# A hybrid encoder layer in float32 on one core: sums, weights and remainders issued at other places

## The chip, the cores and the metric

The kernel runs on one core of a Trainium2 chip. A core has a matrix engine (TensorE, "PE" in the profile), a vector engine (DVE), a scalar engine (ACT), a general engine (GpSimd, "POOL") and an engine that issues DMAs (SyncE, "SP"). Each runs its own queue of instructions in order and waits on semaphores for the others. The metric is the device time of one execution in microseconds (us); the number given for a kernel is the median of its runs.

## The reference

One layer on x of shape 1 x 512 x 1024, all float32:

```python
h = rms_norm(x, attn_norm_g)
xr, gate, q, k, v = jnp.split(h @ w_in, ...)
xr = centred_depthwise_conv(xr, conv_w, conv_b)
h_f = rg_lru(xr, ..., False)
h_b = rg_lru(xr, ..., True)
y_rnn = (h_f + h_b) * jax.nn.gelu(gate)
y_attn = dilated_attention(q, k, v, rel_bias)
mix = jnp.concatenate([rms_norm(y_rnn, norm_rnn_g), rms_norm(y_attn, norm_attn_g)], axis=-1)
x = x + mix @ w_out
h = rms_norm(x, mlp_norm_g)
x = x + jnp.square(jax.nn.relu(h @ w_up)) @ w_down
return rms_norm(x, final_norm_g)
```

d_model is 1024, the hidden width of the MLP 4096; the rnn and the attention group have 512 channels each.

## The kernel before

**Products in three matmuls.** Each float32 operand is split into a rounded part (`hi`, dtype fp32r) and its remainder (`lo`), and a product is hi·hi + hi·lo + lo·hi: three matmuls (`mm3`, lines 329 to 331). For a block of weights, `conv_hi` (line 274) makes `whi` from the raw block on ACT, and `conv_lo` (line 282) makes `wlo` on DVE, as raw minus `whi`. Both are issued three blocks ahead of the block that uses them (`feed`, `dfeed`).

**Seven products for eight.** W_out, W_up and W_down are worked as 2 x 2 quadrants in the manner of Strassen and Winograd: seven products named 11, 21, 22 and s1 to s4, of which s1 to s4 take sums of quadrants. The sums of weights are made by DMA: a quadrant is loaded, and others are accumulated onto it by DMAs that POOL issues (`accum_op=add`). These run on DMA queue q0; the plain loads that SP issues run on q1.

**Order of work.** PE, ACT, DVE and POOL are scheduled by hand: their order is the order of the program text. SP's order is left to the framework's planner. The stages are: x and its columns of W_in (`pxr`), v, the gates, q and k with attention, W_out's rnn half (`wo_thunks`) and attention half (`wo_m`), then for each half of the hidden width W_up (`up_step`, `up_tile`) and W_down (`dmm`).

**x's sums (lines 431 to 441).** x comes in eight row tiles k. DVE adds the squares as tiles arrive (`addsq`, line 374). Before the products of k = 7, PE sums them over the partitions (`col_sums`, line 428), DVE and POOL make the reciprocal root (`rstd_cols`, lines 413 and 416), and PE spreads it to a row later (`rows_of`, line 408), which ACT copies (line 422).

**W_out's attention half (lines 1206 to 1273).** The blocks run in the order `OSEQ` = 11, 21, s2, s3, s4, s1, 22, twelve matmuls each: two row tiles tt, two halves k, three matmuls. For s2, s3 and s4 (`BY_DMA`) the remainder is not made on DVE: ACT writes the negated raw block into a tile, rounded (line 255), and a DMA from POOL adds the raw block to it (line 256), which leaves raw minus its rounded value. This is `conv_neg`; for s2 it is called by `neg_first`, for s3 and s4 inside `conv_hi` of the block before.

**W_down, second half.** 28 blocks j of twelve matmuls: 11 and s1 in turns (j = 0 to 7), s2 and 22 (8 to 15), s3 and 21 (16 to 23), s4 (24 to 27), four blocks q of each. s1's raw tile (`ts`) becomes s2's by one accumulation and s4's by another, each issued in `conv_lo` once the tile has been read (line 311). s3's are loaded by `load_s3` (line 1518) and completed by `sum_s3` (line 1522). The seven products go to PSUM banks that s2, s3 and s4 share with 11; where a product ends, DVE adds the bank to x1n (`add`, line 1657). At j = 8 the last norm's weights `fgt` are loaded as two tiles of 128 rows by 512 (line 1732). `fgt` and most activations are tiles of the ring `g` with 48 slots.

Of the kernel before, what the change touches and what calls it, by code (L numbers as in the profile page):

```python
# [13 lines left out]
FR = mybir.dt.float32r  # L14
# [3 lines left out]
P = 128  # L18
# [91 lines left out]
def hybrid_kernel(ctx: ExitStack, tc, xw, xn, w_in, w_v, w_out, w_up, w_dn, gates, vecs, rel, onehot, fg, out):  # L110
# [121 lines left out]
    def wblock(h, b, q):  # L232
        return w_dn[h, int(b[1]) - 1, (int(b[0]) - 1) * NQ + q]
# [20 lines left out]
    def conv_neg(i, lo):  # L254
        act(lo, raws[i], AF.Copy, scale=-1.0)
        nc.gpsimd.dma_start(lo, raws[i], accum_op=OP.add)
        negs[i] = lo

    def neg_first():
        conv_neg(BY_DMA[0], work.tile([P, 1024], FR, name="tw", tag="tw", bufs=4))  # L260

    def conv_hi(i):
        if i < len(chunks):
            i = swap.get(i, i)
            hi = stream.tile([P, 1024], FR, name="whi", tag="whi", bufs=4)
            if i + 1 in BY_DMA[1:]:
                conv_neg(i + 1, stream.tile([P, 1024], FR, name="wlo", tag="wlo", bufs=4))
            splits[i] = (hi,)
            if i in BY_DMA:
                splits[i] += (negs.pop(i),)  # L270
            if i in ON_DVE:
                nc.vector.tensor_copy(hi, raws[i])
            else:
                act(hi, raws[i], AF.Copy)  # L274

    def conv_lo(i):
        if i < len(chunks):
            i = swap.get(i, i)
            r = raws.pop(i)
            if i not in BY_DMA:  # L280
                lo = stream.tile([P, 1024], FR, name="wlo", tag="wlo", bufs=4)
                nc.vector.tensor_tensor(lo, r, f(splits[i][0]), op=OP.subtract)  # L282
                splits[i] += (lo,)
            c = chunks[i]
            if isinstance(c, tuple) and c[0] in ("o", "r"):
                if c[1][0] != "s":
                    emit_dma()
                elif c == ("r", "s2"):
                    nc.gpsimd.dma_start(r, oblock("21", 0), accum_op=OP.add)
                    raws[C_WO + RSEQ.index("s4")] = r  # L290
            elif isinstance(c, tuple) and len(c) == 4:
                h, kind, f0 = c[:3]
                if kind == "t1" and cq[h, f0, "t2"] not in raws:
                    nc.gpsimd.dma_start(r, ublock(h, "22", f0), accum_op=OP.add)
                    raws[cq[h, f0, "t2"]] = r
                elif kind == "22":
                    t = raws[cq[h, f0, "t3"]]
                    nc.vector.tensor_tensor(t, t, r, op=OP.add)
                elif kind in ("t2", "21"):
                    held[kind] = r  # L300
                    if len(held) == 2:
                        t = held.pop("t2")
                        nc.vector.tensor_tensor(t, t, held.pop("21"), op=OP.add)
                        raws[cq[h, f0, "t4"]] = t
                        emit_dma()
                if kind in ("11", "22"):
                    emit_dma()
            elif isinstance(c, tuple) and c[1][0] == "s":
                nxt = {"s1": ("s2", "22"), "s2": ("s4", "21")}.get(c[1])
                if nxt:  # L310
                    nc.gpsimd.dma_start(r, wblock(c[0], nxt[1], c[2]), accum_op=OP.add)
                    raws[cd_[c[0]] + {"s2": 2 * NQ + 2 * c[2], "s4": 6 * NQ + c[2]}[nxt[0]]] = r
            else:
                emit_dma()

# [12 lines left out]
    def mm3(o, a, b, first, last, on=False):  # L328
        nc.tensor.matmul(o, lhsT=a[0], rhs=b[0], start=bool(first), stop=False, skip_group_check=on)  # L329
        nc.tensor.matmul(o, lhsT=a[0], rhs=b[1], start=False, stop=False, skip_group_check=on)  # L330
        nc.tensor.matmul(o, lhsT=a[1], rhs=b[0], start=False, stop=bool(last), skip_group_check=on)  # L331
# [60 lines left out]
    def hk(k):  # L392
        return (h_hi[:, k, :], h_lo[:, k, :])

    def wk(c, k):
        if c < 3:
            return tuple(t[:, c * P:(c + 1) * P] for t in w3[k])
        hi, lo = splits[c]
        return (hi[:, k * P:(k + 1) * P], lo[:, k * P:(k + 1) * P])
# [11 lines left out]
    def rstd_cols(ssc, n):  # L411
        v = small("rv", 4)
        nc.vector.tensor_scalar(v, ssc, 1.0 / n, EPS, op0=OP.mult, op1=OP.add)
        r = consts.tile([P, 4], FT, name="rcol_%d" % st["rc"])
        st["rc"] += 1
        nc.gpsimd.tensor_tensor(r, v, mhalf, op=OP.pow)
        return r
# [7 lines left out]
    def col_sums(ss, tag):  # L425
        pc = ps_("pcs", tag)
        for tt in range(4):
            nc.tensor.matmul(pc[:, tt:tt + 1], lhsT=ss[:, tt * P:(tt + 1) * P], rhs=ones[:, 0:1], start=True, stop=True)
        return pc[:, 0:4]

    pxr = {t: ps_("pxr", "pj") for t in range(3)}
    for k in range(KD):
        if k == KD - 1:
            rcol = rstd_cols(col_sums(sqx[0], "et"), D)
        if k < 4:
            for i, (a, b) in enumerate(((0, 0), (0, 1), (1, 0))):
                for t in range(3):
                    nc.tensor.matmul(pxr[t], lhsT=wk(t, k)[a], rhs=hk(k)[b], start=k == 0 and i == 0, stop=False)
            continue
        for t in range(3):  # L440
            mm3(pxr[t], wk(t, k), hk(k), False, k == KD - 1)


    relt = consts.tile([NB3, P], FT, name="relt")
# [470 lines left out]
    def o_part(w, tt, k):  # L915
        if w in ("21", "s4"):
            c = slice((w == "s4") * TH + tt * P, (w == "s4") * TH + (tt + 1) * P)
            return [t[:, c] for t in osp[k]]
        return [t[:, k * TH + tt * P:k * TH + (tt + 1) * P] for t in osp[w]]
# [283 lines left out]

    hb, hm, po = {}, {}, {}

    def wo_m(w, tt, k):
        b, tag = {"21": ("c", "pj"), "s1": ("b", "gs"), "22": ("b", "gs")}.get(w, ("a", "et"))
        new = w in ("11", "21", "s1")
        if new and tt == 0 and k == 0:
            po[b] = [ps_("pwo", tag) for _ in range(2)]  # L1210
        hi, lo = splits[C_WA + OSEQ.index(w)]
        sl = slice(k * S, (k + 1) * S)
        mm3(po[b][tt], o_part(w, tt, k), (hi[:, sl], lo[:, sl]), k == 0 and new, k == 1, True)


    def wo_x(w, tt):
# [25 lines left out]
    o_hi2(1)  # L1242
    o_sum("s1", 1)
    o_sum("s2", 1)
    o_his("s2")
    o_sum("22", 1)
    o_lo2(1)
# [20 lines left out]
    for w in OSEQ:  # L1268
        for i in range(4):
            tt, k = i // 2, i % 2  # L1270
            wo_m(w, tt, k)
            if k == 1:
                wo_x(w, tt)
            if i in BES[w]:
                BES[w][i]()
        if w in ("s3", "s4", "s1"):
            load_t(0, {"s3": "t1", "s4": "t2", "s1": "t3"}[w], 4)
# [238 lines left out]
    def load_s3(half, q):  # L1516
        t = work.tile([P, 1024], FT, name="tw", tag="tw", bufs=4)
        nc.sync.dma_start(t, wblock(half, "12", q))
        raws[cd_[half] + 4 * NQ + 2 * q] = t

    def sum_s3(half, q):
        nc.gpsimd.dma_start(raws[cd_[half] + 4 * NQ + 2 * q], wblock(half, "22", q), accum_op=OP.add)

# [2 lines left out]
    for half in range(2):  # L1526
# [170 lines left out]
        for j in range(7 * NQ):  # L1697
            _, w, q = seq[j]
            if q == 0:
                if w in dtag:  # L1700
                    dst[w] = [ps_("pd", dtag[w]) for _ in range(2)]
                else:
                    dst[w] = dst["s1" if w == "22" else "11"]
            if w == "s4" and half == 1:
                break
            for tt in range(2):
                for k2 in range(2):
                    dmm(j, dst[w], tt, k2)
                    dfeed(j, 2 * tt + k2)
                if q == NQ - 1:  # L1710
                    evac(w, tt, dst[w][tt])
            if w == "s1":
                del opsplit[w, q]
                load_s3(half, q)
            if j in S3_AT:
                for x in S3_AT[j]:
                    sum_s3(half, x)
            if half == 0 and j == 16:
                load_t(1, "t1", 0)
            if half == 0 and j == 22:  # L1720
                load_t(1, "t3", 0)
            if half == 0 and j >= HJ:
                h_load(j - HJ)
            if half == 0 and j >= HJ + 2:
                h_hi(*HSEQ[j - HJ - 2])
                h_lo(*HSEQ[j - HJ - 2])
            if half == 1 and j in (4 * NQ, 4 * NQ + 1):
                fin_other(j - 4 * NQ)
            if half == 1 and j == 2 * NQ:
                fgt = [g_("fgt") for _ in range(2)]  # L1730
                for n in range(2):
                    nc.sync.dma_start(fgt[n], bass.AP(tensor=fg.tensor, offset=fg.offset + n * S, ap=[[0, P], [1, S]]))
# [89 lines left out]
```

## Time and profile before

| | |
|---|---|
| median of 3 runs | 529.97 us (529.26 to 530.29) |
| profiled execution | 530.81 us |
| its span, first to last instruction | 529.0 us |
| mean granted TensorE clock | 0.996 |
| PE busy | 519.8 us (98%) |
| DVE, ACT, POOL busy | 431.3, 361.3, 67.5 us |
| q1 (loads), q0 (accumulations) | 74.66 MB, 31.76 MB |

A row of a timeline gives the start in us, the duration in us, engine, line, operation, what is written <- what is read, shape and count; in square brackets the idle time of the engine before it and what ended it. A row of waits gives who waited <- for whom: us in total, times, longest. Matmuls are pipelined, so their durations overlap: how far one starts after another is what counts.

### The profile page before, as it was taken

Reading aid. Unit: us, or ns where it says so; the run is one execution under the profiler, and the core shown is the slowest. Engines: PE = TensorE matmul, PEld = TensorE weight load, DVE = VectorE, ACT = ScalarE, POOL = GpSimd, SP = SyncE. Lnnn points to the kernel's source line nnn. Section 1 sums busy time; section 2 is a strip of 40 time slices with the busy share of each in tenths; the row PEclk is TensorE's granted clock in tenths of the full one; section 3 lists DMA queues with packets and bytes.
Section 4 is the critical chain, followed back from the end, with each engine's and each line's share of the span. In section 5 each row is a group of like instructions: output and inputs, shape, how many; then the busy total and the mean of one; then the engine's idle time right before and its main releaser. Section 6 shows DMA issues by size and latency. Waiting matters only on the chain.

```text
span 529.0 us, 9183 instructions
## 1 busy us (share of the span) xinstructions
PE 519.8 (98%) x3495; PEld 446.4 (84%) x3495; DVE 431.3 (82%) x710; ACT 361.3 (68%) x569; POOL 67.5 (13%) x96
## 2 busy tenths in 40 slices
PE   9999999999999999999999999999999999999995
PEld 8766888787877878899999888889999999887884
DVE  5898588887789897898779987789666978885995
ACT  7567977776878957585578655565476687655654
POOL 3340000001002121001300132001101300322000
PEclk9999999999999999999999999999999999999998
DMA  8788155586478999948495899976977596799504
GB/s 305 259 247 210 40 157 164 169 156 183 82 241 206 276 237 248 356 150 199 119 234 129 244 265 273 287 281 160 315 225 180 130 233 193 179 270 260 166 1 159
DMA packets 35884, 108.30 MB, mean 205 GB/s; under 512 B 4125, under 2 KB 7226, under 8 KB 35840
## 3 DMA queue, kind: packets, MB, share of 16 engines
q1 hardware_dynamic: 26144, 74.66, 41.1%
q0 software_dynamic: 8784, 31.76, 31.9%
q10 hardware_dynamic: 912, 1.30, 1.3%
q8 instruction: 27, 0.44, 0.3%
q14 instruction: 17, 0.14, 0.1%
HBM read 98.24 MB, written 4.21 MB: 194 GB/s over the span
## 4 chain that ended last, share of the span: by engine, by line
PE 81%; issue 7%; DMA 6%; DVE 3%; ACT 1%; POOL 1%; SPq 0%; DVEq 0%; POOLq 0%; ACTq 0%
PE pu L329 10%; PE pu L330 10%; PE pu L331 10%; PE pd L329 8%; PE pd L330 8%; PE pd L331 8%; DMA wraw<-in_w_dn_dram 3%; PE pqk L329 3%; PE pqk L330 3%; PE pqk L331 3%; DMA wlo<-ws 2%; PE pv L329 2%; PE pg L519 1%; PE pv L330 1%; PE pv L331 1%
## 5 line engine op out<-in xcount | busy, mean ns | idle before, releaser
L282 DVE TENSOR_TENSOR wlo<-wraw,whi 128x1024 fp32r<-128x1024 f32 x72 | 87.9, 1221 | 30.0 <-ACT whi L274 29.9
L274 ACT ACTIVATE whi<-wraw 128x1024 fp32r<-128x1024 f32 x69 | 72.9, 1058 | 46.2 <-PE pd L331 18.2
L329 PE MATMUL pd<-whi,ah 128*128 128x512 f32 (+1 forms) x195 | 75.3, 386 | 0.9 <-ACT ah L1434 0.9
L330 PE MATMUL pd<-wlo,ah 128*128 128x512 f32 (+1 forms) x195 | 75.3, 386 | 0.0
L331 PE MATMUL pd<-whi,al 128*128 128x512 f32 (+1 forms) x195 | 75.2, 386 | 0.0
L274 ACT ACTIVATE whi<-tw 128x1024 fp32r<-128x1024 f32 x40 | 42.2, 1058 | 31.2 <-PE pu L330 8.9
L330 PE MATMUL pu<-hl,whi 128*128 128x256 f32 x224 | 63.4, 283 | 0.0
L331 PE MATMUL pu<-hh,wlo 128*128 128x256 f32 x224 | 63.4, 283 | 0.0
L329 PE MATMUL pu<-hh,whi 128*128 128x256 f32 x224 | 63.4, 283 | 0.0
L282 DVE TENSOR_TENSOR wlo<-tw,whi 128x1024 fp32r<-128x1024 f32 x40 | 48.9, 1223 | 15.6 <-ACT whi L274 15.6
L329 PE MATMUL pu<-h2h,whi 128*128 128x256 f32 (+1 forms) x200 | 60.1, 301 | 0.0
L331 PE MATMUL pu<-h2h,wlo 128*128 128x256 f32 (+1 forms) x200 | 60.0, 300 | 0.0
L330 PE MATMUL pu<-h2l,whi 128*128 128x256 f32 (+1 forms) x200 | 60.0, 300 | 0.0
L329 PEld LDWEIGHTS pd<-whi,ah 128*128 128x128 f32 x195 | 36.6, 188 | 8.6 <-ACT ah L1434 1.3
L329 PEld LDWEIGHTS pu<-hh,whi 128*128 128x128 f32 x224 | 43.0, 192 | 0.0
L330 PEld LDWEIGHTS pu<-hl,whi 128*128 128x128 f32 x224 | 43.0, 192 | 0.0
L331 PEld LDWEIGHTS pu<-hh,wlo 128*128 128x128 f32 x224 | 43.0, 192 | 0.0
L331 PEld LDWEIGHTS pd<-whi,al 128*128 128x128 f32 x195 | 36.6, 188 | 7.4
L330 PEld LDWEIGHTS pd<-wlo,ah 128*128 128x128 f32 x195 | 36.6, 188 | 7.2
L274 ACT ACTIVATE whi<-ts 128x1024 fp32r<-128x1024 f32 x24 | 25.5, 1061 | 22.4 <-PE pd L331 19.3
L331 PEld LDWEIGHTS pu<-h2h,wlo 128*128 128x128 f32 x200 | 38.3, 191 | 1.3
L329 PEld LDWEIGHTS pu<-h2h,whi 128*128 128x128 f32 x200 | 38.3, 191 | 1.3
(286 smaller groups left out, 1226.8 us busy)
## 6 DMA issues: line engine op xcount, KB each, us to landing
wraw<-in_w_up_dram SPq DMA_DIRECT2D x25, 512.0 KB
ts<-in_w_dn_dram POOLq DMA_DIRECT2D x24, 512.0 KB, 10.7
wraw<-in_w_dn_dram SPq DMA_DIRECT2D x24, 512.0 KB
tw<-in_w_up_dram SPq DMA_DIRECT2D x15, 512.0 KB
tw<-in_w_up_dram POOLq DMA_DIRECT2D x15, 512.0 KB, 8.9
wraw<-in_w_in_dram SPq DMA_DIRECT2D x13, 512.0 KB
ts<-in_w_dn_dram SPq DMA_DIRECT2D x8, 512.0 KB
tw<-in_w_dn_dram SPq DMA_DIRECT2D x8, 512.0 KB
```

The source lines that it names most:

```text
L274: act(hi, raws[i], AF.Copy)
L282: nc.vector.tensor_tensor(lo, r, f(splits[i][0]), op=OP.subtract)
L329: nc.tensor.matmul(o, lhsT=a[0], rhs=b[0], start=bool(first), stop=False, skip_group_check=on)
L330: nc.tensor.matmul(o, lhsT=a[0], rhs=b[1], start=False, stop=False, skip_group_check=on)
L331: nc.tensor.matmul(o, lhsT=a[1], rhs=b[0], start=False, stop=bool(last), skip_group_check=on)
L519: nc.tensor.matmul(pg[2 * d + j][halves[b ^ d]], lhsT=gwr[t][halves[b], c], rhs=xc[t][halves[b]], start=True, stop=True)
```

## The change

Four places are edited. The sums of x's squares are issued after the products of column tile 0 at k = 7, not before all three. In W_out's attention half, s3's remainder is begun right after the sums for s2 have been issued, and for s2, s3 and s4 the matmuls with the weights' remainder come after those with the rounded weights. In the second half of W_down, the accumulations that make s4's weights leave `conv_lo` and stand at j = 15 to 18 of the program. The load of `fgt` stands at j = 0 instead of j = 8.

```diff
+    def neg_next(i):
+        conv_neg(i, stream.tile([P, 1024], FR, name="wlo", tag="wlo", bufs=4))
+
     def conv_hi(i):
...
-            if i + 1 in BY_DMA[1:]:
-                conv_neg(i + 1, stream.tile([P, 1024], FR, name="wlo", tag="wlo", bufs=4))
+            if i + 1 == BY_DMA[2]:
+                neg_next(i + 1)
...
                 if nxt:
-                    nc.gpsimd.dma_start(r, wblock(c[0], nxt[1], c[2]), accum_op=OP.add)
                     raws[cd_[c[0]] + {"s2": 2 * NQ + 2 * c[2], "s4": 6 * NQ + c[2]}[nxt[0]]] = r
+                    if (c[0], c[1]) != (1, "s2"):
+                        nc.gpsimd.dma_start(r, wblock(c[0], nxt[1], c[2]), accum_op=OP.add)
...
     for k in range(KD):
-        if k == KD - 1:
-            rcol = rstd_cols(col_sums(sqx[0], "et"), D)
...
             mm3(pxr[t], wk(t, k), hk(k), False, k == KD - 1)
+            if k == KD - 1 and t == 0:
+                rcol = rstd_cols(col_sums(sqx[0], "et"), D)
...
-    def wo_m(w, tt, k):
+    def wo_m(w, tt, k, late=False):
...
-        mm3(po[b][tt], o_part(w, tt, k), (hi[:, sl], lo[:, sl]), k == 0 and new, k == 1, True)
+        if not late:
+            mm3(po[b][tt], o_part(w, tt, k), (hi[:, sl], lo[:, sl]), k == 0 and new, k == 1, True)
+            return
+        oh, ol = o_part(w, tt, k)
+        for x in (oh, ol):
+            nc.tensor.matmul(po[b][tt], lhsT=x, rhs=hi[:, sl], start=False, stop=False, skip_group_check=True)
+        if k == 1:
+            for k2 in range(2):
+                nc.tensor.matmul(po[b][tt], lhsT=o_part(w, tt, k2)[0], rhs=lo[:, k2 * S:(k2 + 1) * S],
+                                 start=False, stop=k2 == 1, skip_group_check=True)
...
     o_sum("s1", 1)
     o_sum("s2", 1)
+    neg_next(BY_DMA[1])
     o_his("s2")
...
-            wo_m(w, tt, k)
+            wo_m(w, tt, k, w in ("s2", "s3", "s4"))
...
+    def sum_s4d(q):
+        nc.gpsimd.dma_start(raws[cd_[1] + 6 * NQ + q], wblock(1, "21", q), accum_op=OP.add)
...
-            if half == 1 and j == 2 * NQ:
+            if half == 1 and 15 <= j < 15 + NQ:
+                sum_s4d(j - 15)
+            if half == 1 and j == 0:
                 fgt = [g_("fgt") for _ in range(2)]
```

## The prediction

> **What bounds the kernel now.** I read the busy times of the page first, then TensorE's waits, then the timelines of all engines around each wait.
>
> ```profile
> PE 519.8 (98%) x3495; PEld 446.4 (84%) x3495; DVE 431.3 (82%) x710; ACT 361.3 (68%) x569; POOL 67.5 (13%) x96
> PE pwarm L155 <- DVE epsb L146: 1.0, 1, 1.0
> PE pd L329 <- ACT ah L1434: 0.9, 1, 0.9
> PE pwo L330 <- DMA wlo<-ws: 0.6, 1, 0.6
> PE pcs L428 <- DVE sqx L374: 0.3, 1, 0.3
> ```
>
> TensorE (PE) is busy for 519.8 of 529.0 us. Inside the program it waits three times, once at each of three places, and all four parts of the change are aimed at those places: the sums of x's squares (pcs), W_out's block s3 (pwo), and the first s3 block of the second down projection (pd). The change takes no matmul away, so what can be won is these three stalls and nothing else. How long each is in truth has to be read from start to start, because the ends of matmuls are modelled: matmuls of this size start every 0.227 us (190.55 less 190.33, say, in the rows below).
>
> **Part 1, x's sums one column tile later.** The first fence has PE, the second DVE, POOL and ACT at the same place.
>
> ```profile
> 19.45 0.39 PE L331 MATMUL pxr<-h_hi,w3l 128*128 128x512 f32 x1
> 20.18 1.05 PE L428 MATMUL pcs<-ones,sqx 128*128 128x1 f32 x8 [0.34 <-DVE sqx L374]
> ...
> 23.92 0.60 PE L408 MATMUL prow<-ident,rcol 128*128 128x128 f32 x4
> ```
>
> ```profile
> 18.65 1.48 DVE L374 TENSOR_TENSOR sqx<-sqx 128x512 f32<-128x512 f32 x2
> 21.27 0.16 DVE L413 TENSOR_SCALAR rv<-pcs 128x4 f32<-128x4 f32 x1 [1.15 <-PE pcs L428]
> 21.51 1.97 POOL L416 TENSOR_TENSOR rcol<-rv,mhalf 128x4 f32<-128x4 f32 x1 [10.10 <-DVE rv L413]
> 24.70 0.58 ACT L422 ACTIVATE rrow<-prow 128x512 f32<-128x512 f32 x1
> ```
>
> Before, PE could have started the sums at 19.45 + 0.227 = 19.68, but DVE finishes the last add at 18.65 + 1.48 = 20.13, so they start at 20.18: 0.50 us lost, with a handover of 0.05. After, three matmuls of tile 0 run in between (their operands are made by DVE ahead of that last add), and the sums start at 19.45 + 4 x 0.227 = 20.36, when the add is done. The 0.50 is gone, but the sums are 0.18 later, and a chain hangs on them: rv on DVE, the power on POOL, then the transposes prow on PE. POOL ended at 21.51 + 1.97 = 23.48 and will end at 23.66; with the handover prow may start at 23.71. PE will be there at 23.92 - 0.50 = 23.42. **So a new wait of about 0.29 us takes the place of the old one**, on PE, with everything of PE behind it. The next in the chain, rrow on ACT at 24.70, follows a conversion that keeps ACT busy until then, so it does not move. Net: 23.92 - 23.71 = 0.21 us. Bounds: 0.50 if POOL's power is shorter than it shows (POOL's spans are rough), and -0.2 if the handover from POOL is 0.4 us longer than that from DVE. I take 0.21, since it uses the rows as they stand.
>
> **Part 2, W_out.** Block s3 needs its remainder wlo, which ACT (negation) and POOL (an accumulating DMA) make. The first fence is PE, the second ACT, the third POOL, with the landing times of that DMA.
>
> ```profile
> 190.33 0.39 PE L331 MATMUL pwo<-whi,ol 128*128 128x512 f32 x1
> 190.55 0.39 PE L329 MATMUL pwo<-whi,oh 128*128 128x512 f32 x1
> 191.53 0.50 PE L330 MATMUL pwo<-wlo,oh 128*128 128x512 f32 x1 [0.58 <-DMA wlo<-ws]
> ...
> 194.42 0.39 PE L330 MATMUL pwo<-wlo,oh 128*128 128x512 f32 x1
> ```
>
> ```profile
> 180.33 0.63 ACT L896 ACTIVATE oh<-at 128x512 fp32r<-128x512 f32 x1
> 181.25 0.63 ACT L890 ACTIVATE oh<-osum 128x512 fp32r<-128x512 f32 x1 [0.29 <-DVE osum L909]
> 181.79 1.05 ACT L255 ACTIVATE wlo<-ws 128x1024 fp32r<-128x1024 f32 x1
> ...
> 184.88 1.05 ACT L255 ACTIVATE wlo<-ws 128x1024 fp32r<-128x1024 f32 x1
> ```
>
> ```profile
> 183.13 0.86 POOL L256 DMA_DIRECT2D wlo<-ws  x1 [9.97 <-ACT wlo L255]
> 186.22 0.86 POOL L256 DMA_DIRECT2D wlo<-ws  x1 [2.22 <-ACT wlo L255]
> DMA to landing us min/median/max: 7.8/8.1/8.4
> ```
>
> The stall is 191.53 - 190.55 - 0.227 = 0.75 us. The two DMAs landed at 183.13 + 8.4 = 191.5 (s3) and 186.22 + 7.8 = 194.0 (s4); the second was in time by 0.4 us only, because PE had been held at s3.
>
> The negation for s3 moves ahead of one ACT instruction and into ACT's idle 0.29 us: it can start when the oh of 180.33 ends, near 180.9, 0.9 us sooner, and the DMA with it. Its output slot is no new wait: of the four wlo tiles two belong to W_out's rnn blocks that PE has left by then. What is behind it on ACT, the oh of s2, starts about 0.6 us later and is wanted by PE three blocks on, so that is hidden.
>
> The other half is the order of matmuls. For s2, s3 and s4 the remainders come last within each pair of row tiles: 2 + 2 matmuls with hi, then 2 with lo, six as before, so no time of its own; and each of the 3495 matmuls has a weight load of its own (3495 PEld), so pairing gives nothing to lose. The first use of lo goes from the 2nd to the 5th matmul of a block, 3 x 0.227 = 0.68 us later. For s3: wanted at 190.55 - 0.21 + 4 x 0.227 = 191.25, landed near 190.6; if the DMA did not come sooner at all it would land at 191.5, a wait of 0.25. For s4, without the stall: its first matmul at 190.55 - 0.21 + 12 x 0.227 = 193.06, lo wanted at 193.97, landed at 194.0 if unmoved; its negation starts up to 0.29 sooner, since ACT's idle time is filled. So **s4 is what is late next**, by 0.0 to 0.1 us at worst, as its block loses the delay it had been living on. I take 0.75 for the part; bounds 0.45 and 0.75.
>
> **Part 3, second half's sums and the last norm's weights.** PE, then ACT, DVE, the chain of waits, SP, and the DMA queues (packets, MB, share) in 470 to 486 us:
>
> ```profile
> 488.39 0.39 PE L331 MATMUL pd<-whi,al 128*128 128x512 f32 x1
> 489.64 0.47 PE L329 MATMUL pd<-whi,ah 128*128 128x512 f32 x1 [0.87 <-ACT ah L1434]
> 486.52 1.06 ACT L274 ACTIVATE whi<-wraw 128x1024 fp32r<-128x1024 f32 x1 [4.29 <-DMA wraw<-in_w_dn_dram]
> 487.61 1.23 DVE L282 TENSOR_TENSOR wlo<-wraw,whi 128x1024 fp32r<-128x1024 f32 x1 [4.04 <-ACT whi L274]
> 488.75 0.74 DVE L1657 SCALAR_TENSOR_TENSOR x1n<-pd,nr,x1n 128x512 f32<-128x512 f32 x1
> 470.07 16.35 DMA wraw<-in_w_dn_dram
> 467.43 0.50 SPq L1732 DMA_DIRECT2D fgt<-in_fg_dram x1
> q0 software_dynamic: 640, 2.31, 72.4%
> q1 hardware_dynamic: 638, 1.92, 33.1%
> ```
>
> PE was free at 488.39 + 0.227 = 488.62 and went on at 489.64: 1.02 us lost. The page names ACT, but by the code the first matmul of s3 reuses the PSUM bank of s2, which DVE adds into x1n (488.75 to 489.49); that add stands in DVE's queue behind the remainder of weight block (21, 0) (487.61), which waits for whi on ACT (486.52), which waits for the load wraw. **So the load, 16.35 us for 512 KB, is the cause, through the head of two queues.** PE doesn't need that block until block 17; the harm is in what stands behind it. A landing 1.02 us sooner ends the whole stall.
>
> Why 16 us: for all of 470 to 486 both queues were full and took turns, 640 packets of sums (q0) against 638 of loads (q1), so loads advance at 638 / 16 = 40 packets per us. One load has 144 packets, from this row of 446 to 453 us, where 1.05 MB is two loads of 512 KB:
>
> ```profile
> q1 hardware_dynamic: 288, 1.05, 36.8%
> q0 software_dynamic: 49, 0.14, 10.0%
> ```
>
> So each load takes 144 / 40 = 3.6 us there, and 16.35 is this load and three to four ahead of it. One of those ahead is fgt (467.43), 128 rows of 2 KB, which counts as many packets as a full load. Moved to block 0, near 446 us, it meets DMA engines with half their time free, and the load lands about 3.6 us sooner, near 482.8: over three times what is needed. The s4 accumulations come on top: two of the four stood in q0 ahead of sums that s3 wants. The Trainium skill, page "DMA: Bandwidth & Descriptors", section "Queues, rings and completion order", says that each engine goes round-robin between queues packet by packet; 640 against 638 agrees. By that rule taking sums out of q0 brings a load nothing while q0 stays full, and the sum would be fgt's 3.6 us alone; by shares of bytes it would be up to 3.6 more. Either way the stall is covered. I take 1.02; bounds 0 (nothing sooner) and 1.02.
>
> What it costs: the moved sums have no wait on blocks 15 to 18; POOL runs its queue in order, so they go out right behind the last sum of s3. They must land before s4's weights are converted:
>
> ```profile
> 481.08 1.79 POOL L311 DMA_DIRECT2D ts<-in_w_dn_dram x2 [0.31 <-DVE al L1439]
> ts<-in_w_dn_dram POOLq DMA_DIRECT2D x3, 512.0 KB, 13.7
> 503.55 1.06 ACT L274 ACTIVATE whi<-ts 128x1024 fp32r<-128x1024 f32 x1 [1.14 <-PE pd L331]
> ```
>
> The last sum of before was issued at about 482 and lands 13.7 us later, near 496. The queue holds the same sums in another order, so all are in by then; the first is wanted at 503.55 - 2 = 501.5. Cover: 5 us. If it were gone, each us beyond would cost PE a us. The two loads fgt cost SP 0.5 us each at a place where the queues are half idle: nothing.
>
> **Sum.** 0.21 + 0.75 + 1.02 = 1.98 us. Between the three places PE has no other wait, and loads there are issued when PE's and DVE's progress frees a buffer, so a gain is carried on to the end. Span 529.00 - 1.98 = 527.02; the profiled execution took 530.81, 1.81 more than its span, so 528.83. It was 0.84 slower than the median of three, 529.97, from which I forecast **527.99 us**.
>
> **Rivals.**
> 1. *The load stays late.* SP is the one engine whose order is left to a planner, so fgt may not go out at block 0; and loads of (21, 0) behind two s3 loads may still meet a full q0. Against it: the 3.6 us. Then only parts 1 and 2 pay: 529.97 - 0.96 = 529.0. Chance 0.14.
> 2. *The full stretch moves.* Sums bunched behind s3's keep q0 full, every load at 476 to 495 goes on at 40 packets per us, and the stall comes back at a later DVE add. For it: 640 against 638 packets, turn about. The Trainium skill's page "DMA: Bandwidth & Descriptors", same section, has this turn-taking as its rule. Against it: before, q0 was as full, and the view of waits has one wait of pd, not two. If a stall of 1 us came back and part 1 paid nothing, 529.97 - 0.75 = 529.2. Chance 0.12.
> 3. *Slower: SP is held at fgt.* fgt takes two tiles of ring g (48). If these were not free at block 0, SP would stand at its head, and behind it all weight loads. Counted in the code, 32 tiles are alive there (8 x1n, 11 a, 9 as, 2 ah, 2 al), which speaks against it; so does fgt's issue of before without any wait. Weights are converted three blocks ahead (3 x 12 x 0.227 = 8.2 us), so it costs nothing up to a hold of some 8 us, then a us for each us. At 12 us: 529.97 - 0.96 + 4 = 533. Chance 0.10.
>
> **How the numbers follow.** Forecast 0.64 (own range 527.2 to 528.8: all stalls gone with part 1 at its upper end, 2.27 us, and 0.5 for the spread of medians, half of the runs' 529.26 to 530.29, down to part 2 at its lower end with part 1 at nothing, 1.47, and the same 0.5), rivals 0.14, 0.12, 0.10. The range must take in rivals 1 and 2 with the spread of the medians: 527.2 to 529.8. A measurement here can tell about 0.2%, 1.06 us: faster means below 528.9. Faster: 0.64 and a fifth of rivals 1 and 2, 0.69. Slower 0.10. Within: 0.21.
>
> **What would show it.** Part 1: pcs waits for nothing, prow for POOL by about 0.3 us. Part 2: the negation of s3 at about 180.9, no wait of pwo, or one under 0.3 us at s4. Part 3: fgt issued near 446, the load of (21, 0) in under 13 us, no wait at the first pd of s3; s4 sums issued together after the last of s3, landed before 498. It is wrong if PE has a new wait over 0.5 us anywhere, above all between 450 and 515 us, or if fgt stands on SP with a long wait.

## The result, and the profile after

| | before | after |
|---|---|---|
| median of 22 runs each, side by side | 530.0 us (528.97 to 531.75) | 529.14 us (528.47 to 530.58) |
| ratio | | 0.9984, 95% interval 0.9977 to 0.9991 |
| profiled execution, its span | 530.81, 529.0 us | 529.17, 527.4 us |

The change is faster by 0.16%: 0.9984 x 530.0 is 0.85 us less, with an interval from 0.48 to 1.22. The forecast was 1.98 less; the time is inside its range, and the gain below the 0.2% that it took as the bound of what can be told. The two profiled executions differ by 1.64 us, twice as much as the medians; that difference is the thread of what follows.

The page of after, busy times and the chain that ended last, and below it the one line that the view of PE's waits has beside the first wait of before (who waited <- for whom: us, times, longest):

```profile
PE 519.1 (98%) x3495; PEld 445.8 (85%) x3495; DVE 431.2 (82%) x710; ACT 361.1 (68%) x569; POOL 68.7 (13%) x96
...
PE 97%; DMA 1%; DVE 1%; POOL 0%; ACT 0%; SPq 0%; issue 0%; DVEq 0%; ACTq 0%
```

```profile
PE pxr L440 <- ACT w3h L368: 0.8, 1, 0.8
```

All three waits (pcs, pwo, pd) are gone. There is a new one of 0.8 us at the very start, for x's second tile (pxr), ahead of everything that was edited. The prediction had named a new wait of over 0.5 us anywhere as a sign that it is wrong; a second profile of the changed kernel ("after again", below) lists no such wait, and nothing suggests that this one is of the change's making.

**Part 1 after**, the timeline of PE and then of POOL:

```profile
7.62 0.98 PE L440 MATMUL pxr<-h_hi,w3h 128*128 128x512 f32 x3 [0.76 <-ACT w3h L368]
...
20.71 0.94 PE L432 MATMUL pcs<-ones,sqx 128*128 128x1 f32 x8
...
23.47 0.40 PE L335 MATMUL pxr<-h_hi,wlo 128*128 128x512 f32 x1
23.96 0.65 PE L412 MATMUL prow<-ident,rcol 128*128 128x128 f32 x4
```

```profile
21.94 1.96 POOL L420 TENSOR_TENSOR rcol<-rv,mhalf 128x4 f32<-128x4 f32 x1 [10.56 <-DVE rv L417]
```

The sums pcs wait for nothing. prow starts when POOL's power has ended (21.94 + 1.96 = 23.90, start 23.96), and PE was there 0.49 - 0.227 = 0.27 us before (23.47 to 23.96). So the old wait was exchanged for a new one, as forecast. But prow starts at 23.96, against 23.92 before: the start had held PE up.

**Part 2 after**, the timelines of ACT, POOL, SP and PE, and the landing times of the two accumulating DMAs:

```profile
180.42 0.63 ACT L900 ACTIVATE oh<-at 128x512 fp32r<-128x512 f32 x1
180.96 1.04 ACT L255 ACTIVATE wlo<-ws 128x1024 fp32r<-128x1024 f32 x1
...
182.29 0.87 POOL L256 DMA_DIRECT2D wlo<-ws  x1 [9.71 <-ACT wlo L255]
...
183.58 0.33 SPq L241 DMA_DIRECT2D wraw<-in_w_up_dram  x1
...
191.56 0.62 PE L1225 MATMUL pwo<-wlo,oh 128*128 128x512 f32 x2
```

```profile
DMA to landing us min/median/max: 5.3/6.0/6.6
```

The negation starts at 180.96 where 180.9 was forecast. Its DMA lands in 5.3 us, not in 8.4: at 187.6, four us before the first matmul that wants it (191.56). The issue moved by 0.84 us, the landing by 3.9. What went through the DMA queues in the 3 us from the issue (packets, MB, share of 16 engines), before in 183.1 to 186.1 us and then after in 182.3 to 185.3:

```profile
q1 hardware_dynamic: 90, 0.35, 56.8%
q0 software_dynamic: 15, 0.01, 2.0%
```

```profile
q0 software_dynamic: 112, 0.39, 69.1%
q1 hardware_dynamic: 33, 0.08, 7.1%
```

Before, SP's load on q1 went first and the accumulation on q0 hardly moved; the two did not take turns. After, the accumulation goes first.

**Part 3 after**, the timelines of SP, POOL and ACT, then the DMA queues in 470 to 486 us (packets, MB, share):

```profile
444.98 0.95 SPq L1751 DMA_DIRECT2D fgt<-in_fg_dram  x2
...
469.54 0.33 SPq L241 DMA_DIRECT2D wraw<-in_w_dn_dram  x1
...
478.79 3.93 POOL L1536 DMA_DIRECT2D ts<-in_w_dn_dram  x4
...
482.84 1.06 ACT L277 ACTIVATE whi<-wraw 128x1024 fp32r<-128x1024 f32 x1 [1.14 <-PE pd L335]
```

```profile
q0 software_dynamic: 542, 1.98, 66.4%
q1 hardware_dynamic: 611, 2.23, 36.6%
```

fgt goes out at block 0 without a wait. The load of block (21, 0), issued at 469.54, is there when ACT wants it: the conversion at 482.84 waits for PE, where before it waited for the load (at 486.52). So the load took 13.3 us at most, where it took 16.35. The four s4 sums go out together, 478.79 to 482.7; by the trace the last of them starts at 480.95 and lands 15.8 us later, at 496.8.

Nearly all that the prediction said of the places was there; whether the load took under 13 us, as it said, the trace doesn't tell. What was wrong is the amount.

### The profile page after: what moved, and what is told of

Read it like the earlier page. It is cut to its first block, busy times and chain, and to the rows that moved or that the text cites. A ratio compares the mean times of both kernels' runs of the same rounds, so it can differ in the third digit from the quotient of the medians.

```text
span 527.4 us, 9182 instructions
## 1 busy us (share of the span) xinstructions
PE 519.1 (98%) x3495; PEld 445.8 (85%) x3495; DVE 431.2 (82%) x710; ACT 361.1 (68%) x569; POOL 68.7 (13%) x96
## 3 DMA queue, kind: packets, MB, share of 16 engines
HBM read 98.24 MB, written 4.21 MB: 194 GB/s over the span
## 4 chain that ended last, share of the span: by engine, by line
PE 97%; DMA 1%; DVE 1%; POOL 0%; ACT 0%; SPq 0%; issue 0%; DVEq 0%; ACTq 0%
PE pu L333 10%; PE pu L334 10%; PE pu L335 10%; PE pd L333 10%; PE pd L335 10%; PE pd L334 10%; PE pqk L333 3%; PE pqk L335 3%; PE pqk L334 3%; PE pt L845 2%; PE pav L932 2%; PE pv L333 2%; PE pg L523 1%; PE pn L791 1%; PE pv L334 1%; PE pv L335 1%
```

## The experiments

Two theories. **Fixed**: each stall is in every execution as the first profile shows it, and something new gives half of it back. **Come and go**: when a DMA lands, and so how long PE stalls, differs from execution to execution; the first profile of before was a slow draw, and the sum of its stalls isn't what the kernel usually loses.

### The kernel before once more, and each part alone

The kernel before, with no edit:

> The kernel before, unchanged. Theory A (the three stalls of the first profile, 0.50 + 0.75 + 1.02 us, are there in every execution, and the gain is lost somewhere in the changed kernel): this profile shows the same three waits within 0.1 us each. Theory B (the profiled execution was a slow draw, 530.81 against a median of 530.0, because the landing of DMAs differs from execution to execution): one or more of the three waits is shorter by 0.3 us or more, and TensorE's start on x differs too. Time: ratio 1.000 in both.

Part 1 alone:

```diff
-        if k == KD - 1:
-            rcol = rstd_cols(col_sums(sqx[0], "et"), D)
...
+            if k == KD - 1 and t == 0:
+                rcol = rstd_cols(col_sums(sqx[0], "et"), D)
```

> x's sums one column tile later, alone. Theory A: -0.2 us, sums without a wait, and a wait of 0.3 us at the row of roots. Theory B, for this part: what TensorE loses at the start (a wait for x's second tile, 0.76 us in the changed kernel's profile, none in the one before) makes it arrive later at the sums, so that there was little to win: 0.0 to -0.2 us. The waits at W_out's s3 (up to 0.75) and at the first s3 block of the down projection (up to 1.0) stay.

Part 2 alone (both halves):

```diff
-            if i + 1 in BY_DMA[1:]:
+            if i + 1 == BY_DMA[2]:
...
+    neg_next(BY_DMA[1])
...
-            wo_m(w, tt, k)
+            wo_m(w, tt, k, w in ("s2", "s3", "s4"))
```

> W_out alone: s3's negation sooner and remainders last for s2, s3, s4. Theory A: -0.75 us. Theory B: what the wait at s3 is in a usual execution, between 0 and 0.75. In both: no wait of the W_out products in the profile, the waits at x's sums and at the down projection stay.

Part 3 alone (both halves):

```diff
+                    if (c[0], c[1]) != (1, "s2"):
+                        nc.gpsimd.dma_start(r, wblock(c[0], nxt[1], c[2]), accum_op=OP.add)
...
+            if half == 1 and 15 <= j < 15 + NQ:
+                sum_s4d(j - 15)
-            if half == 1 and j == 2 * NQ:
+            if half == 1 and j == 0:
```

> Second half's sums for s4 and the last norm's weights at other blocks, alone. Theory A: -1.0 us. Theory B: what the wait at the first s3 block is in a usual execution, between 0 and 1.0. In both: no wait there in the profile, the load of weight block (21, 0) is in under 13 us, the waits at x's sums and W_out's s3 stay.

| | median (range), us | ratio to before, 95% interval |
|---|---|---|
| before, in the same comparison (35 runs) | 529.51 (528.62 to 531.14) | |
| before again | 529.95 (528.55 to 532.44) | 1.0008, 0.9994 to 1.0022 |
| part 1 | 529.28 (528.89 to 532.55) | 1.0001, 0.9987 to 1.0015 |
| part 2 | 529.13 (528.55 to 530.76) | 0.9996, 0.9984 to 1.0007 |
| part 3 | 528.92 (528.27 to 529.32) | 0.9987, 0.9977 to 0.9996 |

Part 3 alone brings most of what the whole change brings. Its 11 runs spread over 1.05 us, the 35 of before over 2.52. The views of waits tell more; first that of before again, then that of part 2:

```profile
PE pwo L330 <- DMA wlo<-ws: 0.5, 1, 0.5
PE pd L329 <- ACT ah L1434: 0.3, 1, 0.3
```

```profile
PE pd L332 <- ACT ah L1447: 0.9, 1, 0.9
```

The same code as before shows no wait at pcs now, and one of 0.3 us at pd in place of 0.9. Part 1's view lists none at pwo or pd, which it doesn't touch, and part 3's none at pcs or pwo, though both theories had these stay; in part 2's, pd is as bad as in the first profile. That speaks for stalls that come and go.

### The two halves of part 3

fgt alone, the other half being left as before:

```diff
-            if half == 1 and j == 2 * NQ:
+            if half == 1 and j == 0:
```

> Of the change only the two loads fgt at block 0; the s4 sums stay where they were. Theory 'turns' (the two DMA queues take turns packet by packet, so a load is late by the packets of its own queue ahead of it): fgt was 144 packets in front of the load of block (21, 0), so with it gone that load lands about 3.6 us sooner, in about 12 to 13 us instead of 16, and no pd of s3 waits; time as with the whole of part 3, 0.5 to 0.7 us under before. Rival 'sums' (the sums crowd the loads out, so it is the two s4 sums in the other queue that count): the load still takes over 15 us and pd waits 0.3 to 1.1 us in the profile, time within 0.2 us of before.

The s4 sums alone (in the expectation, "block 6" is the place of before, j = 8):

```diff
+                    if (c[0], c[1]) != (1, "s2"):
+                        nc.gpsimd.dma_start(r, wblock(c[0], nxt[1], c[2]), accum_op=OP.add)
...
+            if half == 1 and 15 <= j < 15 + NQ:
+                sum_s4d(j - 15)
```

> Of the change only the four s4 sums together behind the last sum of s3; fgt stays at block 6. Theory 'turns': the sums' queue is as full as before at 470 to 486 us, loads go on at 40 packets per us with fgt among them, the load of block (21, 0) takes 15 us or more, pd waits 0 to 1.1 us as in the executions of before, time within 0.2 us of before. Rival 'sums': the load takes under 13 us, pd waits for nothing, time 0.5 to 0.7 us under before.

Each half ends the stall by itself: neither profile has a wait at pd, and in both the conversion of block (21, 0) waits for PE and not for the load. The timelines of ACT, fgt alone first, then the s4 sums alone:

```profile
482.29 1.06 ACT L274 ACTIVATE whi<-wraw 128x1024 fp32r<-128x1024 f32 x1 [1.14 <-PE pd L331]
```

```profile
482.62 1.06 ACT L274 ACTIVATE whi<-wraw 128x1024 fp32r<-128x1024 f32 x1 [1.14 <-PE pd L332]
```

The queues in 470 to 486 us, in the same order:

```profile
q0 software_dynamic: 596, 2.18, 68.3%
q1 hardware_dynamic: 599, 2.19, 36.7%
```

```profile
q0 software_dynamic: 465, 1.71, 55.6%
q1 hardware_dynamic: 938, 2.87, 47.5%
```

Without fgt the queues still take turns (596 to 599), and the load is early because less stands ahead of it. Without the two s4 sums q0 runs empty for part of the time (2 packets start on it from 478 to 480 us by the trace, beside 292 on q1), and the loads get 938 packets through in place of 638. So 'turns' was right for fgt and wrong for the sums: it took for granted that q0 stays full. 'sums' was wrong in holding fgt for harmless. In time, fgt alone has a median of 528.87 us (528.17 to 529.73) and the s4 sums alone 528.90 (528.34 to 529.74), against 529.25 of before. The ratios are 0.9997 (0.9989 to 1.0006) and 0.9990 (0.9980 to 1.0000): for fgt alone the time by itself tells nothing, and neither median reaches the 0.5 to 0.7 us under before that was expected, so that the verdict on both halves rests on the profiles.

### A third profile of before

No edit:

> The kernel before once more, for a third profile of it and as a measure of what a difference between two like kernels may be. Theory 'intermittent' (the stalls at pcs, pwo and pd depend on when DMAs land, which differs from execution to execution): ratio within 0.15% of 1, and a profile in which the three stalls are again of other sizes than 0.50, 0.75 and 1.02 us, some of them 0. Rival 'fixed': 0.50, 0.75 and 1.02 within 0.1 us.

529.58 us (528.67 to 532.41), ratio 1.0005 (0.9988 to 1.0021). Its view of waits lists none of pcs, pwo or pd. PE's timeline has a small one at W_out, at s4 and not at s3; below it stands ACT's timeline with the conversion of block (21, 0):

```profile
192.74 0.47 PE L329 MATMUL pwo<-whi,oh 128*128 128x512 f32 x1
193.35 0.50 PE L330 MATMUL pwo<-wlo,oh 128*128 128x512 f32 x1
```

```profile
484.79 1.06 ACT L274 ACTIVATE whi<-wraw 128x1024 fp32r<-128x1024 f32 x1 [3.46 <-DMA wraw<-in_w_dn_dram]
```

s3's DMA had landed in 7.1 us, so that s4 was the late one, by 193.35 - 192.74 - 0.227 = 0.38 us: what the prediction had as late next. The load landed near 484.8, 1.7 us sooner than in the first profile, and pd lost 0.2 us in place of 1.02. 'Come and go' (in the expectation, 'intermittent') holds.

### The two halves of part 2

The negation sooner, the order of matmuls left:

```diff
-            if i + 1 in BY_DMA[1:]:
+            if i + 1 == BY_DMA[2]:
...
+    neg_next(BY_DMA[1])
```

> Of the change only the negation for W_out's block s3 sooner; the remainders stay in their places among the matmuls. Theory 'ahead of the load': the accumulating DMA now goes out before the load of the next weight block (182.3 against 183.5 us) and not behind it, so that it lands in about 5.3 us instead of 7.0 to 8.4, near 187.5, three us before it is wanted; s4's lands near 192.5, before it is wanted near 193; first pwo to first pxt takes 15.26 to 15.32 us. Rival 'as predicted': the landing moves by the 0.9 us of the issue alone, to 189 to 190.6, and s4's stays at 192.6 to 194.0 and costs up to 0.5 us. Time 0.2 to 0.5 us under before in the one case, 0 to 0.4 in the other.

The remainders late, the negation left:

```diff
-            wo_m(w, tt, k)
+            wo_m(w, tt, k, w in ("s2", "s3", "s4"))
```

> Of the change only the remainders of s2, s3 and s4 last within their blocks; the negation stays where it was. Both theories: the DMA for s3 goes out at about 183 behind the load and lands in 7.0 to 8.4 us, 189.5 to 191.5, and is wanted near 191.2: a wait of 0 to 0.3 us at s3 and none or 0.1 at s4; first pwo to first pxt 15.26 to 15.6 us. Time 0.1 to 0.4 us under before. If lateness did not matter at all, as where the sums of the page are off by more than this, 15.7 us or more as in before.

The landing times, the negation sooner first, then the remainders late:

```profile
DMA to landing us min/median/max: 5.3/5.9/6.6
```

```profile
DMA to landing us min/median/max: 7.0/7.3/7.6
```

Neither waits at pwo. With the negation sooner, the DMA goes out at 181.82 and SP's load of the next block at 183.11, by their timelines; before, they went out at 183.13 and 183.49, and POOL's issuing instruction ran until 184.0. In all six profiles with the sooner negation s3's DMA lands in 5.3 us; in the eight without, in 7.0 to 8.4. So 'ahead of the load' holds: the issue moved by 0.9 us and the landing by up to 4. That the load is what it passes is read from the order of issues and from the packets shown above; why q0 hardly moves even after 184.0 stays open, and a kernel with the load moved instead was not tried. Of the late remainders the profile shows little: s3's DMA landed at 182.57 + 7.0 = 189.6, in time for the old order too, whose place for it is the second matmul of s3, at 190.23; s4's landed at 185.66 + 7.6 = 193.3, 0.1 us behind the old place at 193.20.

In time the two are 529.32 us (528.48 to 532.61; ratio 0.9998, 0.9984 to 1.0011) and 529.27 (528.70 to 530.14; 0.9995, 0.9986 to 1.0004), against 529.61: nothing that can be told. The profiled execution of the first was one of its longest, 532.61 us, and shows one way in which the kernels without part 3 come to such a tail. The chain that ended last, then PE's timeline, then windows (us, PE busy, PEld, DVE, ACT, POOL, granted clock, DMA share, GB/s):

```profile
469.06 17.56 DMA wraw<-in_w_dn_dram
```

```profile
487.38 0.39 PE L334 MATMUL pd<-whi,al 128*128 128x512 f32 x1
489.85 0.47 PE L332 MATMUL pd<-whi,ah 128*128 128x512 f32 x1 [2.08 <-ACT ah L1438]
...
490.65 0.63 PE L332 MATMUL pd<-whi,ah 128*128 128x512 f32 x1
491.07 0.63 PE L333 MATMUL pd<-wlo,ah 128*128 128x512 f32 x1
```

```profile
488.00:490.60 2.60, 0.75 (x3) 0.67 (x4) 2.60 (x4) 1.77 (x3) 0.00 (x0) 1.00 1.07 279
490.60:494.00 3.40, 3.40 (x9) 2.64 (x8) 3.40 (x5) 0.24 (x1) 0.00 (x0) 0.50 1.05 260
494.00:496.00 2.00, 2.00 (x10) 1.65 (x9) 1.17 (x3) 2.00 (x5) 0.00 (x0) 1.00 0.83 256
```

The load took 17.56 us, PE stood still for 489.85 - 487.38 - 0.227 = 2.24 us, and right after that the granted clock was 0.50 for 3.4 us: matmuls start every 0.42 to 0.43 us. The down projection lost 3.93 us in all. Four of the executions of the kernels without part 3 took 532.4 us or more, and of all whose clock is on record only these have a mean granted clock of 0.995 or less. So a slow stretch is likely in all four; where it fell, only this profile shows.

### The wait at prow, and the changed kernel again

The whole change, and prow one group of matmuls later:

```diff
-    xmm((0,))
+    xmm((0, 1))
     rstd = row_tile(rcol, "et")
...
-    xmm((1, 2, 3, 4))
+    xmm((2, 3, 4))
```

> The whole change, and the transposes of the root row (prow) behind one more group of matmuls. If the wait of 0.27 us at prow is in every execution, as the rows of after have it (the chain DVE, POOL, PE is all compute, no DMA in it): prow waits for nothing and the time is 0.2 to 0.3 us under that of the changed kernel, 528.6 to 528.9. Rival: at the start PE is bound by the landing of x, by 0 to 0.9 us that differ from execution to execution, and the wait at prow is only what the start leaves: no difference within 0.15 us.

The same kernel again, and the changed kernel, side by side:

> The whole change with the transposes of the root row one group of matmuls later, beside the changed kernel on one chip. If the 0.27 us at prow is in every execution: median 0.15 to 0.3 us below the changed kernel's, no wait at prow. If it is only what the start leaves: within 0.15 us of it.

> The changed kernel once more, beside the three below on one chip. Theory 'intermittent': PE's time in W_out (first pwo to first pxt) and in the second down projection (first to last pd) is again 15.29 and 233.00 us within 0.05, since all that could be late there lands with room; what differs is the first stretch alone (first pxr to first pbias, 46.2 to 47.4 us so far). Time 528.6 to 529.2, ratio 0.998 to 0.999. Rival: the stalls of the two later stretches come back in some executions, 0.2 us or more over those sums.

PE's timeline with prow later:

```profile
23.37 0.39 PE L335 MATMUL pxr<-h_hi,wlo 128*128 128x512 f32 x1
23.60 0.60 PE L412 MATMUL prow<-ident,rcol 128*128 128x128 f32 x4
```

The wait is gone (23.60 - 23.37 = 0.23), where the changed kernel has it in both its profiles, at 0.27 us. The medians: 528.55 us (528.24 to 529.07), ratio 0.9983 (0.9974 to 0.9992) in the first comparison; in the second 528.90 (528.09 to 529.61), 0.9986 (0.9976 to 0.9995), beside 528.94 (528.42 to 529.66), 0.9987 (0.9979 to 0.9996), for the changed kernel. It beats the kernel before both times; whether it beats the changed kernel can't be told: the two medians are 0.04 us apart where 0.15 to 0.3 was expected, and 0.27 us is 0.05%. The changed kernel's second profile lost nothing in the later stretches, as 'intermittent' had it.

### All profiles by stretch

What PE lost, from the starts of its matmuls in all fourteen profiles, in us. "pcs" and "prow" is how much over 0.227 they start after the matmul before; "x" is the time from the first pxr to the first pbias; "W_out" from the first pwo to the first pxt, less the 15.26 of the fastest; "W_down" from the first to the last pd (the second half's W_up lies in between), less 233.00.

| | x | pcs | prow | W_out | W_down | span |
|---|---|---|---|---|---|---|
| before | 47.18 | 0.50 | 0 | 0.66 | 1.13 | 529.0 |
| before again | 46.88 | 0 | 0 | 0.54 | 0.58 | 528.2 |
| before, third | 46.37 | 0.18 | 0 | 0.46 | 0.31 | 527.3 |
| part 1 | 46.94 | 0 | 0.27 | 0.28 | 0.21 | 527.5 |
| part 2 | 47.17 | 0 | 0 | 0.03 | 1.29 | 528.6 |
| negation sooner | 46.84 | 0.21 | 0 | 0.03 | 3.93 | 530.8 |
| remainders late | 46.51 | 0.42 | 0 | 0 | 0.30 | 527.0 |
| part 3 | 46.92 | 0.06 | 0 | 0 | 0 | 527.0 |
| fgt alone | 46.61 | 0 | 0 | 0.03 | 0 | 526.8 |
| s4 sums alone | 46.86 | 0.57 | 0 | 0 | 0 | 527.1 |
| after | 47.39 | 0 | 0.27 | 0.03 | 0 | 527.4 |
| after again | 46.59 | 0 | 0.27 | 0.03 | 0 | 526.8 |
| prow later | 46.18 | 0 | 0 | 0 | 0 | 526.5 |
| prow later, again | 46.13 | 0 | 0 | 0 | 0 | 526.3 |

"x" holds pcs and prow. Outside these stretches only the start of the first pxr differs, from 4.53 to 4.84 us; all else agrees within 0.07, so that the rows account for the spans. W_down loses 0.21 to 3.93 in all seven profiles without part 3 or a half of it, and nothing in all seven with it. W_out loses 0 to 0.66 in the seven without part 2 or a half of it, 0.03 at most in the seven with it. But of those seven only the four that also lack part 3 lose 0.28 to 0.66; in the three with part 3 or a half of it W_out loses 0.03 at most too, with the same DMAs issued in the same order up to 188 us. Whether that is chance is not shown. pcs loses 0 to 0.57 in the nine that have it where before had it; with part 1 it loses nothing, but prow loses 0.27 each time, until it too is moved.

And x differs by 0.8 us among kernels with the same code there. Most of that is the clock at the start. The first three matmuls of pxr, in part 2's profile and in that of the remainders late:

```profile
4.69 1.62 PE L441 MATMUL pxr<-h_hi,w3h 128*128 128x512 f32 x3
4.76 0.94 PE L438 MATMUL pxr<-h_hi,w3h 128*128 128x512 f32 x3 [0.17 <-ACT e L166]
```

In the first, matmuls start every 0.43 us up to 6.96, as in the slow stretch above, and every 0.23 from 7.31 on; the trace's record of the granted clock begins there, with full clock from 7.19 us. In the second full clock is on record from 4.21 us. In all fourteen it comes between these two. Half of the time from the first pxr to full clock may be counted as lost, 0 to 1.25 us; x less that loss, pcs and prow is 45.9 to 46.3 us in thirteen profiles, and 47.1 in after, with its wait of 0.76 us for x's second tile. The wait at pcs goes with the clock too: of the nine profiles with the old order, where full clock came before 6.0 us it is 0.18 to 0.57, where it came later 0 to 0.06, as PE then comes late itself. So it isn't the landing of DMAs alone that makes this wait come and go.

That the stall of W_down is the load's, and how it comes and goes, is seen when the start of the conversion of block (21, 0) on ACT is counted from the first pd:

| | conversion after first pd, us | W_down's loss, us |
|---|---|---|
| part 1 | 197.33 | 0.21 |
| remainders late | 197.42 | 0.30 |
| before, third | 197.44 | 0.31 |
| before again | 197.70 | 0.58 |
| before | 198.27 | 1.13 |
| part 2 | 198.43 | 1.29 |
| negation sooner | 199.49 | 3.93 |

Up to 198.43 the loss is the conversion's lateness over 197.13, us for us; the last has 2.36 us by that, and the rest, 1.57, is near the 1.7 that half the clock for 3.4 us costs. In the seven profiles with part 3 or a half of it the conversion starts at 195.13 every time, and waits for PE.

## Why the prediction was right in kind and more than twice too large

**The step that failed is the sum**, 0.21 + 0.75 + 1.02 = 1.98: each term was the stall of one execution, taken for that of all. The working even said that the profiled execution was 0.84 us slower than the median of three, and took that for a shift to be carried along unchanged; most of it was the stalls themselves: by the table this execution lost 2.29 us at pcs, in W_out and in W_down, and the two other profiles of before 1.12 and 0.95. (One end of its own range is off as well: 529.97 - 1.47 + 0.5 is 529.0, not 528.8; nothing hangs on it.) What each term measured:

- *Part 1, 0.21.* The shape was exact: 0.50 less a new wait at prow of 0.29, which measured 0.27. But the 0.50 is 0, 0.18, 0.21, 0.42, 0.06, 0, 0.57 and 0 in the eight other profiles with that order, 0.22 on average with its own, and the 0.27 comes each time. So the part is worth 0.22 - 0.27 = -0.05. Alone it measured a ratio of 1.0001.
- *Part 2, 0.75.* The seven profiles without it lose 0.28 us on average. With it, or with either half, 0.03 at most is lost; that the late remainders are needed for this no profile shows. The negation brought more than was forecast (a landing 4 us sooner, not 0.9), but there was only so much to win. Alone: 0.9996, which its interval can't tell from nothing.
- *Part 3, 1.02.* The median of the seven profiles without it is 0.58 us, the mean 1.11 with the long one. It removes all of it. Alone: 0.9987, or 0.69 us of 529.51.

-0.05 + 0.28 + 0.58 is 0.81 us, and 0.85 was measured. That the two are so close is in part a matter of choice: with medians throughout the sum is -0.09 + 0.28 + 0.58 = 0.77, and with means throughout 1.34, above the interval of 0.48 to 1.22. In the means the execution that lost 3.93 weighs one in seven, while executions of 532.4 us and more are 4 of 197 of the kernels without part 3 (70 of the experiments, 127 of before in the comparisons). Without any profile, the ratios of the three parts alone multiply to 1.0001 x 0.9996 x 0.9987 = 0.9984, that of the whole change, though the interval of each is 0.19% to 0.28% wide.

**The mechanisms.** The wait named as ACT's at pd was the load's, two queues further back, as the prediction read it: the loss follows the load us for us in the table above, and taking packets from either queue ends it. On the s4 sums the prediction had left open what they would bring: nothing while q0 stays full. q0 didn't stay full: with the s4 sums moved and fgt left, 938 packets of loads went through beside 465. The Trainium skill, page "DMA: Bandwidth & Descriptors", section "Queues, rings and completion order", has the round-robin go between the queues that an engine has work for; that run agrees, and with 596 to 599 beside fgt's, the two cases are seen side by side.

**The rivals.** The load didn't stay late, and SP wasn't held at fgt (issued at 444.98 with no wait). The full stretch did not move: q0 carries 542 packets in 470 to 486 us after, 640 before, and PE has no wait behind it. More than half of the forecast gain was missing, by none of the rivals; it had not been there in most executions.

**What the medians leave out.** The change takes away the long executions most of all. Over 530.0 us are 2 of 88 executions of the kernels with part 3 or a half of it (after among them), 16 of 70 of those without, and 41 of 127 of the kernel before in the comparisons.

## What to carry to other kernels

A stall behind a DMA was a draw here (0.21 to 3.93 us in W_down): profile the same kernel two or three times, take the median loss of the stretch, and only then size the gain. When a profiled execution is slower than the median, look for the surplus in such stalls first, and in the clock at the start. The wait on a compute chain (pcs to prow) was the same in all three profiles that have it, so trading a wait of 0.22 us on average for a fixed one of 0.27 was no gain. What a DMA costs depends on what is issued around it: an issue 0.9 us sooner, well ahead of a load, brought the landing forward by up to 4 us.

## What was not expected of the hardware

- A pause of PE of 2.24 us was followed by 3.4 us at a granted clock of 0.50 and matmuls every 0.43 us, so that the execution lost 3.93 us in place of 2.24. Pauses of 1.03 and 1.08 us (before, part 2) have no such stretch behind them. The Trainium skill, page "TensorE: Matmul & The Clock Gate", section "What's actually happening", names an idle window of about 3.4 us; the length of the slow stretch agrees with that, but a pause of two thirds of it was enough here. The trace has full clock from 5.89 to 490.58 us, 484.69 us or 142 times 3.413, and in the thirteen other traces for 518.83 us, 152 times 3.413, each time. So the clock changed on a grid of 3.413 us, and the whole pause (487.6 to 489.85) lay in one step of it, 487.17 to 490.58; in part 2 the pause of 1.08 lay across two.
- The same accumulation of 512 KB from one SBUF tile to another landed in 5.3 us six times out of six when issued 1.3 us ahead of a load, and in 7.0 to 8.4 us, eight times out of eight, when issued 0.36 us ahead of it.
